# Loading four gate weights before the last blocks of a down projection, and spreading a norm's row one block later

## The chip, the cores and the metric

The kernel runs on one core of a Trainium2 chip. The metric is device time in microseconds, the median of repeated executions. Five engines work beside each other, each through its own queue in order: PE (TensorE) multiplies matrices, DVE (VectorE) and ACT (ScalarE) work on vectors, POOL (GpSimd) adds, and SP (SyncE) issues the transfers between HBM and the on-chip memory. An instruction waits until what it needs has been produced on the other engines, and everything behind it in the same queue waits with it.

## The reference, cut to what matters

One decoder layer on x of 1024 tokens by 1024 features: a gated feed-forward block, a token mixer (a short convolution and a windowed attention, each with a sigmoid gate), a second feed-forward block, and a last norm. The place of the change is the seam between the first block and the mixer:

```python
h = modulate(rms_norm(x, g_ffn1[l]), sh1, sc1)
x = x + 0.5 * gt1[:, None, :] * swiglu(h, w1_gu[l], w1_down[l])

h = modulate(rms_norm(x, g_mix[l]), sh2, sc2)
proj = h @ w_in[l]
b_g, c_g, u, q, k, v, z_conv, z_attn = jnp.split(proj, IN_OFFSETS, axis=-1)
...
merged = jax.nn.sigmoid(z_conv) * y_conv + jax.nn.sigmoid(z_attn) * y_attn
```

The norm needs the mean square over all 1024 features of a token, so it can be finished only when the last row block of x has been updated.

## The kernel before, in words

**Layout.** Features lie on the 128 partitions, tokens along the free axis. x is kept as 8 row blocks (db = 0..7) by 2 halves of 512 tokens (h = 0, 1), each a 128x512 tile. Every matrix product is done in float32 precision with three passes over split operands: each operand is cut into a rounded high part and the remainder, and `mm3` issues high by high (L138), high by low (L140) and low by high (L142). A split costs one ACT instruction for the high part (CAST, L106) and one DVE subtraction for the remainder (L107), for every 128x512 piece. Large products use a scheme of seven products in place of eight; their matmuls all stand at L195.

**Weights.** `load_w` loads a 128x1024 block into one of four raw buffers ("wr", L114) and splits it into two parts tiles, two CASTs and two L107. Parts tiles come from a pool of eight ("w"), or, where a list of tiles is handed over, from the large pool of 28 tiles ("t") that also holds the inputs of the products. A raw buffer is free for the next load when both of its halves are split.

**The seam.** After `down_seven` has done 20 of the 22 row blocks of the down projection w1_down, `down_part` does the last two for each half h: eight blocks db of six matmuls each, every one followed on DVE by `add_gated` (L569), which adds the block into x. `end1` follows each: ACT squares the block (L312 for the first, L315 for the others), POOL sums the squares (L319), and SP writes the block to HBM ("spill"). When the first half is summed, `rstd` adds over the partitions with four tiny matmuls (L328), and computes the reciprocal root on ACT and DVE (L253 to L260). `spread` turns the result into a 128x512 row with four more (L269). Both are called while PE is in the blocks of the second half: the statistic after db = 3, the row after db = 4. `mix_h` then makes the mixer's input for eight blocks: a DVE multiplication (L275), the high part and the full value on ACT (L279, L285) and the low part on DVE (L290).

**The four plain gates.** Four of the sixteen gate tiles are computed plainly, by `some_gates`: first all four on half 0 (`k` runs over the 8 input blocks; 4 x 3 matmuls for each k), then on half 1. In the first of these loops the statistic of half 1 is asked for at k = 2 and its row at k = 4, and `mix_h` for half 1 follows. Their four weight blocks are loaded by `load_w` just ahead of `some_gates` in the text. After them the first `seven_stream` begins, whose weights are split by `seven_weights` (L154 to L163 make sums of blocks, L106 and L107 split them), and which takes in blocks of the adaLN computation (L225, each on a raw buffer of its own load of "wada").

**Order.** PE's instructions are issued in the order of the text. Those of DVE, ACT, POOL and SP around the seam are ordered by a scheduler, which also hands out the buffers.

Of the kernel before, what the change touches and what calls it, by code (L numbers as in the profile page):

```python
# [35 lines left out]
def tile_macaron_layer(  # L36
# [32 lines left out]
    def nm(s):  # L69
        uid[0] += 1  # L70
        return f"{s}_{uid[0]}"
# [7 lines left out]
    def tile_t(dt=F32R, shape=(P, 2, HALF)):  # L79
        return act.tile(list(shape), dt, tag="T", name=nm("t"), bufs=28)  # L80
# [31 lines left out]
    def load_st(src):  # L112
        st = wgt.tile([P, 1024], F32, tag="wr", name=nm("wr"), bufs=4)
        nc.sync.dma_start(st[:, : src.shape[1]], src)  # L114
        return st
# [15 lines left out]
    def load_w(src, lo_engine=nc.vector, tiles=None):  # L131
        return Weights(load_st(src), src.shape[1], lo_engine, tiles)
# [132 lines left out]
    def spread(rr):  # L265

        pb = bank()
        for b in range(rr.shape[1]):
            mm(pb[:, b * P : (b + 1) * P], rr[:, b : b + 1].to_broadcast([P, P]), ident,  # L269
               start=True, stop=True)  # L270
        return pb
# [360 lines left out]
    with tc.tile_pool(name="f1", bufs=2) as tmp:  # L632
# [158 lines left out]
        def mix_h(pb, db, h):  # L791
            tt[db][h] = tile_t()
            hh2[db][h], hl2[db][h] = pair_of(tt[db][h])
            modulated(xT[db][h], pb, 1, db, hh2[db][h], hl2[db][h], xT[db][h])
            if h == 1 and db < 4:
                nc.sync.dma_start(h12[db], f32(tt[db][h]))

        wd_ = [load_w(w1d[2 * NCH, dq]) for dq in range(2)]

        def end1(h):  # L800
            def after(db):
                stats[h].add(xT[db][h])
                nc.sync.dma_start(spill[db][h], xT[db][h])
                if h == 1 and db == 3:
                    rs[0] = stats[0].rstd()
                if h == 1 and db == 4:
                    pb = spread(rs[0])
                    for d in range(KT):
                        mix_h(pb, d, 0)
            return after  # L810
# [91 lines left out]
            def c21(self, oa):  # L902
                self.done(self.i2, 0, oa, -1.0)


        plain = [(1, 0), (1, 1), (0, 0), (0, 1)]
        wg = [load_w(wz[which, db]) for which, db in plain]

        def some_gates(idx, h, between=lambda k: None):
            banks = [bank() for _ in idx]  # L910
# [514 lines left out]
```

## Time and profile before

| | before |
|---|---|
| median of 3 runs | 2264.24 us (2263.83 to 2266.13) |
| the profiled execution, whole time | 2263.03 us |
| its span in the profile | 2261.3 us |
| PE busy | 2196.2 us, 97% of the span |
| DVE busy | 1680.0 us, 74% |
| ACT busy | 1061.2 us, 47% |
| POOL busy | 382.3 us, 17% |
| the seam: last down blocks and plain gates | from 671.5 to 752.6 us of the span |

A row of a timeline gives the start and the length in microseconds, the engine, the line of the kernel, the instruction, what it writes and reads, how many were merged into the row (x3), and in brackets how long the engine had been idle before it and who ended that idle time. Matmuls overlap in the pipeline: a 128x512 matmul is shown 0.39 us long, and the next one starts 0.23 us after it. Rows of the windows view give, for a stretch of time, the busy time of each engine with its number of instructions, and behind POOL the clock that was granted to PE (1.00 is full), the share of the DMA engines and the rate.

### The profile page before, as it was taken

The page shows a single profiled execution, that of the slowest core. Times are in us where ns is not written, and L with a number is a line of the kernel's source. Part 1 is how long each engine was busy: PE and PEld are TensorE (multiplying, and loading weights), DVE is VectorE, ACT ScalarE, POOL GpSimd, SP SyncE. Part 2 cuts the span into 40 slices and gives each one's busy share as a digit, 9 for nine tenths or more (in the row PEclk, how much of TensorE's full clock was granted, in tenths as well). Part 3 has the DMA queues.
Part 4 walks back from the last instruction along what each step waited for, and adds up shares of the span by engine and source line. Part 5 has one row for each costly group of instructions (what it writes and reads, how often), then busy time and mean ns, then how long its engine had stood idle before and what let it go on. Part 6 is the DMA issues. An engine that isn't in the chain of part 4 may idle for free.

```text
span 2261.3 us, 30036 instructions
## 1 busy us (share of the span) xinstructions
PE 2196.2 (97%) x10392; PEld 1842.2 (81%) x10392; DVE 1680.0 (74%) x2978; ACT 1061.2 (47%) x2091; POOL 382.3 (17%) x429
## 2 busy tenths in 40 slices
PE   5899999999998999999999999999999999999997
PEld 4688888888886888888899998888888888888886
DVE  8897778768768877777477888555786777676876
ACT  4554444444445533433476656124554444454443
POOL 3000000004553000000344333001100000002644
PEclk9999999999999999999999999999999999999998
DMA  8264456499833534543312125444243553399932
GB/s 319 79 219 165 143 203 214 159 397 314 298 102 117 177 107 145 159 140 126 125 57 65 34 91 205 125 165 149 66 142 116 181 186 122 118 331 343 342 110 75
DMA packets 146456, 380.58 MB, mean 168 GB/s; under 512 B 20352, under 2 KB 22528, under 8 KB 146304
## 3 DMA queue, kind: packets, MB, share of 16 engines
q1 hardware_dynamic: 141696, 370.28, 46.9%
q0 software_dynamic: 4608, 8.39, 2.1%
q8 instruction: 81, 1.33, 0.2%
q14 instruction: 71, 0.58, 0.1%
HBM read 269.56 MB, written 109.05 MB: 167 GB/s over the span
## 4 chain that ended last, share of the span: by engine, by line
PE 89%; DVE 7%; issue 1%; DMA 1%; ACT 1%; POOL 1%; SPq 0%; POOLq 0%; DVEq 0%; ACTq 0%
PE ps L195 63%; PE ps L138 6%; PE ps L142 6%; PE ps L140 6%; PE ps L977 1%; PE ps L975 1%; PE ps L976 1%; DVE w L107 1%; PE ps L1031 1%; DVE t L225 1%; PE ps L1074 1%; DMA wr<-in_w2d_dram 1%; DVE t L107 1%; POOL s L319 1%; DVE x L569 1%
## 5 line engine op out<-in xcount | busy, mean ns | idle before, releaser
L195 PE MATMUL ps<-t,w 128*128 128x512 f32 x6468 | 1468.6, 389 | 4.4 <-DVE r L405 3.0
L195 PEld LDWEIGHTS ps<-t,w 128*128 128x128 f32 x6468 | 1213.6, 188 | 258.8 <-DVE r L405 4.9
L106 ACT CAST w<-wr 128x512 fp32r<-128x512 f32 (+1 forms) x412 | 250.7, 613 | 480.6 <-PE ps L195 365.1
L107 DVE TENSOR_TENSOR w<-wr,w 128x512 fp32r<-128x512 f32 (+1 forms) x396 | 299.7, 764 | 136.3 <-ACT w L106 134.9
L515 POOL TENSOR_TENSOR x<-x,g 128x512 f32<-128x512 f32 x96 | 145.6, 1531 | 1060.0 <-DMA t<-hs 940.7
L106 ACT CAST w<-ws 128x512 fp32r<-128x512 f32 x231 | 143.9, 623 | 251.4 <-PE ps L195 202.7
L140 PE MATMUL ps<-t,w 128*128 128x512 f32 (+1 forms) x528 | 205.5, 389 | 4.9 <-DVE t L290 4.9
L107 DVE TENSOR_TENSOR w<-ws,w 128x512 fp32r<-128x512 f32 x231 | 161.5, 703 | 39.1 <-ACT w L106 38.6
L138 PE MATMUL ps<-t,w 128*128 128x512 f32 (+1 forms) x400 | 156.9, 392 | 6.2 <-ACT t L279 6.2
L142 PE MATMUL ps<-t,w 128*128 128x512 f32 (+1 forms) x400 | 155.0, 388 | 2.0 <-DVE w L107 2.0
L140 PEld LDWEIGHTS ps<-t,w 128*128 128x128 f32 x528 | 100.9, 191 | 27.1 <-DVE t L290 7.6
L344 DVE TENSOR_TENSOR x<-x,x 128x512 fp32r<-128x512 f32 x161 | 102.8, 688 | 3.0 <-ACT x L343 2.8
L225 DVE CUSTOM_DVE_ANT_0 wr<-wr,crow_act,v 128x1024 f32<-128x1024 f32 x56 | 71.8, 1283 | 35.9 <-DMA wr<-in_wada_dram 35.8
L343 ACT CAST x<-x 128x512 fp32r<-128x512 f32 x161 | 88.8, 623 | 19.3 <-DVE x L431 8.0
L138 PEld LDWEIGHTS ps<-t,w 128*128 128x128 f32 x400 | 76.8, 192 | 23.2 <-ACT t L279 8.9
L319 POOL TENSOR_TENSOR s<-s,q 128x512 f32<-128x512 f32 (+1 forms) x48 | 56.8, 1186 | 201.1 <-ACT q L315 199.6
L142 PEld LDWEIGHTS ps<-t,w 128*128 128x128 f32 x400 | 76.7, 192 | 17.3 <-DVE w L107 2.4
L569 DVE SCALAR_TENSOR_TENSOR x<-ps,mods,x 128x512 f32<-128x512 f32 (+1 forms) x104 | 72.8, 707 | 22.7 <-PE ps L195 12.3
L975 PE MATMUL ps<-w,t 128*128 128x384 f32 x256 | 88.2, 345 | 1.2 <-DVE vt L1000 1.2
L107 POOL TENSOR_TENSOR w<-wr,w 128x512 fp32r<-128x512 f32 (+1 forms) x16 | 21.5, 1355 | 398.6 <-ACT w L106 398.6
L977 PE MATMUL ps<-w,t 128*128 128x384 f32 x256 | 85.7, 335 | 0.0
L976 PE MATMUL ps<-w,t 128*128 128x384 f32 x256 | 85.7, 335 | 0.0
(152 smaller groups left out, 2801.7 us busy)
## 6 DMA issues: line engine op xcount, KB each, us to landing
t<-hs SPq DMA_DIRECT2D x140, 512.0 KB, 10.1
hs<-x SPq DMA_DIRECT2D x277, 256.0 KB, 4.6
wr<-in_wada_dram SPq DMA_DIRECT2D x56, 512.0 KB, 3.8
wr<-in_w1gu_dram SPq DMA_DIRECT2D x44, 512.0 KB, 4.5
wr<-in_w2gu_dram SPq DMA_DIRECT2D x44, 512.0 KB, 3.6
wr<-in_wbcu_dram SPq DMA_DIRECT2D x24, 512.0 KB, 4.1
wr<-in_w1d_dram SPq DMA_DIRECT2D x22, 512.0 KB, 7.6
wr<-in_w2d_dram SPq DMA_DIRECT2D x22, 512.0 KB, 7.5
```

Source lines behind the costliest of these rows:

```text
L106: nc.scalar.copy(hi, src)
L107: lo_engine.tensor_tensor(lo, src, f32(hi), op=ALU.subtract)
L138: mm(o, wh, xh, start=start, stop=False)
L140: mm(o, wh, xl, start=False, stop=False)
L142: mm(o, wl, xh, start=False, stop=stop)
L195: mm(o, a, b, start=first, stop=last, skip_group_check=True)
L344: nc.vector.tensor_tensor(f32r(t), t, f32(hi), op=ALU.subtract)
L515: nc.gpsimd.tensor_tensor(dst, dst, r, op=ALU.add)
L569: nc.vector.scalar_tensor_tensor(out=dst, in0=src, scalar=gate[:, db : db + 1], in1=dst if base is None else base, op0=ALU.mult, op1=ALU.add,)
L975: mm(o[:, :384], xh, wh, start=k == 0, stop=False)
L976: mm(o[:, :384], xh, wl, start=False, stop=False)
L977: mm(o[:, :384], xl, wh, start=False, stop=k == KT - 1)
```

## The change

The list of the four plain gates and their `load_w` calls stand ahead of the definition of `end1`, so they are recorded before `down_part` runs; the last two of the four are given two tiles each of the large pool "t". And the row of half 0 is spread after block db = 5 of half 1, where it was db = 4; the statistic is still taken after db = 3.

```diff
         wd_ = [load_w(w1d[2 * NCH, dq]) for dq in range(2)]
+        plain = [(1, 0), (1, 1), (0, 0), (0, 1)]
+        wg = [load_w(wz[which, db], tiles=[tile_t(), tile_t()] if i > 1 else None)
+              for i, (which, db) in enumerate(plain)]
 
         def end1(h):
             def after(db):
...
                 if h == 1 and db == 3:
                     rs[0] = stats[0].rstd()
-                if h == 1 and db == 4:
+                if h == 1 and db == 5:
                     pb = spread(rs[0])
                     for d in range(KT):
                         mix_h(pb, d, 0)
...
-        plain = [(1, 0), (1, 1), (0, 0), (0, 1)]
-        wg = [load_w(wz[which, db]) for which, db in plain]
```

The scheduler puts the moved instructions in new places on DVE, ACT and SP; POOL keeps its order, and behind about the first two products of `seven_stream` all engines stand as before. Three places matter.

On DVE, the end of the seven products and the beginning of the last down blocks, of the changed kernel. The names that start with t_56 are the parts of the third and fourth gate weight, wr_5655 and wr_5663 their raw buffers, wr_6335 the raw buffer of the first weights of `seven_stream`; x_3953 is row block 0 of half 0:

```order
L569 SCALAR_TENSOR_TENSOR x_3957<-ps_5513,mods,x_3957 128x512
L107 TENSOR_TENSOR t_5653<-wr_5655,t_5653 128x512
L569 SCALAR_TENSOR_TENSOR x_3958<-ps_5522,mods,x_3958 128x512
L107 TENSOR_TENSOR t_5654<-wr_5655,t_5654 128x512
...
L107 TENSOR_TENSOR t_5661<-wr_5663,t_5661 128x512
L107 TENSOR_TENSOR t_5662<-wr_5663,t_5662 128x512
...
L154 TENSOR_TENSOR ws_6340<-wr_6335 128x512
L569 SCALAR_TENSOR_TENSOR x_3959<-ps_5463,ngate_3951,x_3959 128x512
...
L569 SCALAR_TENSOR_TENSOR x_3953<-ps_5670,mods,x_3953 128x512
```

Before, none of these L107 stood here (the third and fourth weight were split at the statistic of half 0 and in the middle of `mix_h`), and L154 stood behind the third L569 of the last blocks. In the built program wr_5655, wr_5663 and wr_6335 are now one and the same raw buffer, used one after the other: each load waits for the second L107 of the one before it.

On DVE, the statistic of half 0; ps_5779 and ps_5811 are its sums, x_3965 and x_3966 are blocks 4 and 5 of half 1. Before:

```order
L107 TENSOR_TENSOR w_5960<-wr_5958,w_5960 128x512
L107 TENSOR_TENSOR w_5961<-wr_5958,w_5961 128x512
L254 TENSOR_SCALAR nv_5784<-ps_5779 128x4
L255 RECIPROCAL nr_5785<-nt_5786 128x4
L569 SCALAR_TENSOR_TENSOR x_3965<-ps_5793,mods,x_3965 128x512
L256 SCALAR_TENSOR_TENSOR nt_5786<-nr_5785 128x4
L259 TENSOR_TENSOR nt_5786<-nt_5786,nv_5784 128x4
L260 SCALAR_TENSOR_TENSOR nr_5785<-nt_5786,nr_5785 128x4
```

and of the changed kernel:

```order
L107 TENSOR_TENSOR w_6337<-wr_6333,w_6337 128x512
L107 TENSOR_TENSOR w_6342<-ws_6340,w_6342 128x512
L254 TENSOR_SCALAR nv_5816<-ps_5811 128x4
L255 RECIPROCAL nr_5817<-nt_5818 128x4
L161 TENSOR_TENSOR ws_6353<-ws_6348,wr_6333 128x512
L569 SCALAR_TENSOR_TENSOR x_3965<-ps_5825,mods,x_3965 128x512
L256 SCALAR_TENSOR_TENSOR nt_5818<-nr_5817 128x4
L569 SCALAR_TENSOR_TENSOR x_3966<-ps_5837,mods,x_3966 128x512
L259 TENSOR_TENSOR nt_5818<-nt_5818,nv_5816 128x4
L260 SCALAR_TENSOR_TENSOR nr_5817<-nt_5818,nr_5817 128x4
```

Two splits still stand ahead of the statistic (now of `seven_stream`'s weights), and inside it stand two instructions more: L161, and the L569 of the block that PE does later.

On DVE, between the statistic of half 1 and its modulation, of the changed kernel; nothing stood between L260 and L275 before:

```order
L260 SCALAR_TENSOR_TENSOR nr_6008<-nt_6009,nr_6008 128x4
L225 ISA wr_6493,mods<-wr_6493,crow_act,v 128x1024
L225 ISA mods 128x1
L225 ISA wr_6496,mods<-wr_6496,crow_act,v 128x1024
L225 ISA mods 128x1
L275 SCALAR_TENSOR_TENSOR u_6046<-x_3961,amod,ps_6040 128x512
```

A third L225, on wr_6490, stands ahead of the last L290 of half 0. The raw buffers wr_6490, wr_6493 and wr_6496 are one and the same, so the loads run one after the other, each behind the L225 of the one before.

## The prediction

> **What bounds the kernel now.** I read the page first: its busy times, then the chain that ended last.
>
> ```profile
> PE 2196.2 (97%) x10392; PEld 1842.2 (81%) x10392; DVE 1680.0 (74%) x2978; ACT 1061.2 (47%) x2091; POOL 382.3 (17%) x429
> PE 89%; DVE 7%; issue 1%; DMA 1%; ACT 1%; POOL 1%; SPq 0%; POOLq 0%; DVEq 0%; ACTq 0%
> ```
>
> PE sets the time, so the change is worth only what PE loses at the seam. The windows view over the seam, and over four stretches in it, shows how much that is:
>
> ```profile
> 671.50:752.63 81.13, 73.63 (x322) 59.60 (x320) 68.19 (x105) 51.11 (x87) 20.69 (x15) 0.96 0.36 127
> 691.00:694.50 3.50, 1.18 (x9) 1.18 (x10) 2.20 (x7) 0.74 (x2) 2.88 (x3) 1.00 0.40 109
> 694.50:698.00 3.50, 3.50 (x10) 2.75 (x10) 3.40 (x6) 2.62 (x5) 0.16 (x1) 0.54 0.30 115
> 708.00:711.70 3.70, 1.22 (x10) 0.79 (x8) 3.50 (x3) 0.00 (x0) 2.87 (x2) 1.00 0.30 121
> 711.70:715.10 3.40, 3.40 (x11) 2.75 (x11) 0.74 (x5) 0.26 (x1) 0.00 (x0) 0.52 0.00 0
> ```
>
> PE is idle for 81.13 - 73.63 = 7.5 us, and twice, after a stretch in which it hardly worked, its clock is half (0.54, 0.52). The timeline of PE names the waits:
>
> ```profile
> 688.30 1.05 PE L328 MATMUL ps<-ones,s 128*128 128x1 f32 x8 [0.31 <-POOL s L319]
> 693.32 1.16 PE L269 MATMUL ps<-ident,nr 128*128 128x128 f32 x8 [2.47 <-DVE nr L260]
> 700.67 0.51 PE L140 MATMUL ps<-t,w 128*128 128x512 f32 x1 [0.23 <-DVE t L290]
> 705.23 0.50 PE L142 MATMUL ps<-t,w 128*128 128x512 f32 x1 [2.00 <-DVE w L107]
> 711.00 1.13 PE L328 MATMUL ps<-ones,s 128*128 128x1 f32 x8 [2.48 <-POOL s L319]
> 713.00 0.63 PE L142 MATMUL ps<-t,w 128*128 128x512 f32 x1
> 713.42 0.63 PE L138 MATMUL ps<-t,w 128*128 128x512 f32 x1
> 719.06 1.05 PE L269 MATMUL ps<-ident,nr 128*128 128x128 f32 x8
> 752.63 22.60 PE L195 MATMUL ps<-t,w 128*128 128x512 f32 x99
> ```
>
> The change aims at the 2.47 (the row of half 0) and the 2.00 (the split of the fourth gate weight). The wait behind them, 2.48 until 711.00, is for the statistic of half 1. Between 719.06 and 752.63 PE waits no more. So everything depends on when that second statistic can start: a wait that goes away ahead of 711.00 is only waited out there. A full-speed matmul takes 22.60/99 = 0.228 us, so a block of six is 1.37; at half clock the step is 713.42 - 713.00 = 0.42, and some eight such matmuls behind each low stretch cost 8 x 0.2 = 1.6.
>
> **The chain to the second statistic.** From the row of half 0 it runs over L275 on DVE, eight pairs on ACT, the last squares on ACT, and their sums on POOL:
>
> ```profile
> 694.60 4.70 DVE L275 SCALAR_TENSOR_TENSOR u<-x,amod,ps 128x512 f32<-128x512 f32 x7 [1.33 <-PE ps L269]
> 695.38 0.72 ACT L279 ACTIVATE t<-u,mods 128x512 fp32r<-128x512 f32 x1 [2.13 <-DVE u L275]
> 705.02 1.67 ACT L315 ACTIVATE q<-x 128x512 f32<-128x512 f32 x3
> 705.78 5.17 POOL L319 TENSOR_TENSOR s<-s,q 128x512 f32<-128x512 f32 x3 [11.12 <-ACT q L315]
> ```
>
> From 693.32 to 711.00 that is 17.68 us, and PE's own work is shorter. Three sums stand at its end, 5.17/3 = 1.72 each.
>
> **The change part by part.**
>
> *The splits in front of the last blocks.* Four L107 and four CASTs now run while the seven products end, with three more DVE instructions (L154, L158, L163). Nothing is added to the total; what counts is when L154 lets x go on.
>
> ```profile
> 655.83 0.68 DVE L107 TENSOR_TENSOR w<-wr,w 128x512 fp32r<-128x512 f32 x1
> 656.54 0.33 SPq L114 DMA_DIRECT2D wr<-in_wz_dram  x1
> DMA to landing us min/median/max: 3.4/3.6/3.8
> 661.34 1.17 DVE L107 TENSOR_TENSOR w<-wr,w 128x512 fp32r<-128x512 f32 x1
> 666.11 2.99 POOL L515 TENSOR_TENSOR x<-x,g 128x512 f32<-128x512 f32 x2 [2.45 <-DVE x L569]
> 673.14 0.75 DVE L569 SCALAR_TENSOR_TENSOR x<-ps,mods,x 128x512 f32<-128x512 f32 x1
> 676.95 0.96 DVE L154 TENSOR_TENSOR ws<-wr 128x512 f32<-128x512 f32 x1 [0.40 <-DMA wr<-in_wz_dram]
> 681.23 3.48 DVE L569 SCALAR_TENSOR_TENSOR x<-ps,mods,x 128x512 f32<-128x512 f32 x5
> 682.84 10.02 POOL L319 TENSOR_TENSOR s<-s,q 128x512 f32<-128x512 f32 x7 [2.08 <-ACT q L315]
> ```
>
> Three loads follow each other in one raw buffer. wr_5655 is issued at 656.54 as the load in its place was, and lands 3.6 later, at 660.1. Its CASTs (two, 0.6 each) and its two L107, of 1.17 each beside POOL and with an L569 between them, end at about 663.6. wr_5663 then lands at 667.3, and its splits end at about 669.7. wr_6335 is issued then and lands at 673.4. L154, L158, L163, two L569 and one L107 stand ahead of x_3953: six times 0.66 gives 677.4, against 673.14 before. POOL's last instructions for the seven products lie ahead of that. The blocks of x then go 0.66 us apart, the first square is summed from about 679.5, and seven sums of 1.33 end at 688.8. Before, four sums of 1.33 from 682.84 ended at 688.2. So the statistic starts **0.6 us later**. PE does not stall on its accumulators ahead of that: block 8 (682.4) needs the one that x_3953 frees at 678.1. Bounds: none, if the loads take 3.4; 2 us, if each of the three takes 0.4 more and the L107 beside POOL 0.3 more.
>
> *The row after db = 5.*
>
> ```profile
> 688.70 3.03 DVE L107 TENSOR_TENSOR w<-wr,w 128x512 fp32r<-128x512 f32 x2
> 691.65 0.15 DVE L254 TENSOR_SCALAR nv<-ps 128x4 f32<-128x4 f32 x1
> 693.10 0.16 DVE L260 SCALAR_TENSOR_TENSOR nr<-nt,nr 128x4 f32<-128x4 f32 x1
> ```
>
> Again two L107 hold DVE until 691.65 (at 1.5 each beside POOL), so the 0.6 us of the statistic are hidden: ACT's root would be ready at 691. Then L161 comes in (0.7 alone, 1.4 beside POOL, whose sums for half 1 still run), and L569 of block 5, which PE ends at 688.9 + 0.9 + 2 x 1.37 = 692.6. L260 ends at 694.1 to 695.0; I take 694.9, as POOL is busy. PE has then waited about 2.3 us, nearly the 2.47 of before, and L269 comes at 695.0, **1.7 us later** than 693.32, with 1.37 us more of PE's work behind it.
>
> *From the row to the second statistic.* The x of block 5 is already there, so two squares are left behind the eight pairs instead of three: 17.68 - 1.72 = 15.96, and 695.0 + 15.96 = 710.96. **The second statistic starts at 710.96 against 711.00.** With the lower end of L260 (694.1) it is 710.1; with the loads at their upper end 712.
>
> *The removed wait.* With the fourth weight split early, PE does not stop at L142. It starts k = 0 when L290 of block 0 has run: seven L275 from 696.3, one L569 and L290 give 702.3, where it was 700.67. k = 0 and 1 are 24 matmuls, 5.5 us, to 707.7. The 2.00 us are gone, and PE waits 3.2 us for the statistic instead of 2.48.
>
> *The clock.* There are now two long pauses, 698.7 to 702.3 and 707.7 to 711. If the first one halves the clock, k = 0 and 1 take 1.6 us longer, in time that is waited out anyway, the second pause is 1.6 us and may leave the clock full: 1.6 us won. If not, the second halves it as before. I count half of it, **-0.8 us**, with 0 and -1.6 as its ends. [...]
>
> *L225 ahead of the second modulation.*
>
> ```profile
> 706.36 5.13 DVE L290 SCALAR_TENSOR_TENSOR t<-u,mods,t 128x512 fp32r<-128x512 f32 x3
> L225 DVE CUSTOM_DVE_ANT_0 wr<-wr,crow_act,v 128x1024 f32<-128x1024 f32 x56 | 71.8, 1283 | 35.9 <-DMA wr<-in_wada_dram 35.8
> wr<-in_wada_dram SPq DMA_DIRECT2D x56, 512.0 KB, 3.8
> 720.15 5.36 DVE L275 SCALAR_TENSOR_TENSOR u<-x,amod,ps 128x512 f32<-128x512 f32 x8 [6.85 <-PE ps L269]
> ```
>
> The first L225 stands ahead of the last L290 of half 0, which ended at 706.36 + 5.13 = 711.5 before; I put it at 711.3 to 712.6. Then load (3.8), L225 (1.3), load, L225: 12.6 + 2 x 5.1 = 722.8, where L275 could start at 720.15. The first low part of half 1 (5.36 and 0.75 later) is there at 728.9; PE reaches half 1 at 719.9 + 48 x 0.228 = 730.8. So 2.7 us late are hidden under 4.6; without that cover they would cost one for one. Behind it DVE has as much left as before, and `seven_stream`'s first weights are split already.
>
> **Sum.** -0.04 for the second statistic and -0.8 for the clock: **-0.8 us**. The profiled execution (2263.03, span 2261.3) becomes 2262.2. It is 1.2 below the median of the runs, 2264.24, so the median becomes **2263.4**. Its own range: -0.9 - 1.6 at the best, +1 with late loads and +1.6 for a second slow stretch, rounded to 2261 to 2267.
>
> **Rivals.** One: *the removed waits are a gain as they stand*, 2.47 + 2.00 + 2.48 and one slow stretch of 1.6, 8.5 us: 2255.7. For it speaks that all of them are on the chain of PE; against it, that the second statistic starts from the row of half 0, and that two instructions now stand inside that row's computation. Chance 0.05. Two: *serial loads hold DVE*. Three loads in one raw buffer stand ahead of the first statistic, two ahead of the second modulation. It decides from the point where the first three are over 1 us late in sum (the cover that L254 gives), or the two over 1.9. With the 7.6 us that the page gives for a load beside heavy traffic,
>
> ```profile
> wr<-in_w1d_dram SPq DMA_DIRECT2D x22, 512.0 KB, 7.6
> ```
>
> it is 3 x 4.0 - 1 = 11 us: 2275. Against it: the loads of in_wz here took 3.8 at most, and the DMA share of the whole seam is 0.36. Chance 0.06. Three: *the change does not do what it says*: the row moves by a block of PE's work, 1.37 us, two splits still stand ahead of the statistic, and the wait at L142 is only moved; the chain then ends 1.4 later: 2265.6. Chance 0.12. The forecast keeps 0.77.
>
> **How the numbers follow.** A measurement of this kernel tells 0.2%, 4.5 us, from no change. The forecast and rival three lie within it. Faster takes rival one and 0.01 of the rest, 0.06; slower is 0.05, most of rival two; the same, 0.89. Eight in ten lie from 2260.5 to 2267.0: the forecast's own range with half a microsecond for the runs below it, and rival three inside.
>
> **What would show it.** L142's wait for L107 at the gates is gone. The two CAST and L107 pairs of the third and fourth weight lie ahead of 671.5. L154 waits for its load until about 673.4, and x_3953 follows at 677. L269 of half 0 starts at 694 to 695.5, with a wait of 1.5 to 2.4 us. PE then waits about 3.5 us for L290, and once more for POOL at L328, which starts at 710 to 712. The second L275 starts at 722 to 723.5, and PE does not wait for it. Wrong would be: L328 ahead of 708, or PE idle after 719, or a load of the seam over 4.5 us.

## The result and the profile after

The changed kernel takes **2268.81 us** (median of 22 runs, 2266.30 to 2274.26) against 2264.60 us of the kernel before, in as many runs beside it. The ratio is 1.0020, with a 95% interval of 1.0014 to 1.0027: the change costs 3 to 6 us. The prediction was 2263.4 us and no difference that can be told. The profiled execution has a span of 2267.2 us, 5.9 us more than before.

By the page of the changed kernel PE is busy for 2196.8 us, as before (2196.2). Its share of the chain that ended last falls from 89% to 87%, DMA goes from 1% to 2% and DVE from 7% to 8%:

```profile
PE 87%; DVE 8%; DMA 2%; issue 1%; ACT 1%; POOL 1%; SPq 0%; POOLq 0%; DVEq 0%; ACTq 0%
```

The timeline of PE at the seam, changed kernel: its four waits of over 0.3 us, the tiny matmuls of the statistics (L328) and rows (L269), and the first product of `seven_stream` behind the seam:

```profile
671.13 3.04 PE L195 MATMUL ps<-t,w 128*128 128x512 f32 x12 [3.00 <-DVE x L569]
690.33 0.95 PE L328 MATMUL ps<-ones,s 128*128 128x1 f32 x8
697.38 2.08 PE L269 MATMUL ps<-ident,nr 128*128 128x128 f32 x8 [3.22 <-DVE nr L260]
705.64 0.50 PE L140 MATMUL ps<-t,w 128*128 128x512 f32 x1 [2.57 <-DVE t L290]
714.88 1.87 PE L328 MATMUL ps<-ones,s 128*128 128x1 f32 x8 [3.72 <-POOL s L319]
724.28 1.05 PE L269 MATMUL ps<-ident,nr 128*128 128x128 f32 x8
757.84 22.38 PE L195 MATMUL ps<-t,w 128*128 128x512 f32 x98
```

The first row is new: 3.00 us in which PE, ahead of the last twelve matmuls of the seven products, waits for DVE to add a block into x. The 2.00 us at L142 are gone, as the change meant, but the waits for the row and for the second statistic have grown from 2.47 to 3.22 and from 2.48 to 3.72.

To compare executions, times are taken from one event ahead of the seam, an addition of DVE in the seven products, some 60 us earlier. Before and after:

```profile
612.91 1.40 DVE L569 SCALAR_TENSOR_TENSOR x<-ps,ngate,x 128x512 f32<-128x512 f32 x2
```
```profile
612.32 1.40 DVE L569 SCALAR_TENSOR_TENSOR x<-ps,ngate,x 128x512 f32<-128x512 f32 x2
```

From there to the first product of `seven_stream` it was 752.63 - 612.91 = 139.72 us, and is 757.84 - 612.32 = 145.52: **5.8 us more, nearly the whole of the 5.9 that the span gained**. (These are two single executions; the medians lie 4.2 us apart.) Cut at the starts of L328 and L269, the parts were 75.39 to the first statistic, 5.02 to its row, 17.68 to the second statistic, 8.06 to its row, and 33.57 to the end. The change moved them by +2.62, +2.03, -0.18, +1.34 and -0.01.

**The first loss.** The chain of waits of the changed kernel shows what stands behind the 3.00 us (start, length, and the engine or transfer that the chain runs through):

```profile
663.21 3.51 DMA wr<-in_wz_dram
666.79 0.63 ACT t L106
667.45 1.07 DVE t L107 x2
668.73 1.01 issue
669.74 0.68 DVE w L107
670.42 0.67 DVE x L569
671.13 3.04 PE ps L195 x12
```

The load of the fourth weight, the second of the three that share one raw buffer, lands at 666.7. Its splits hold DVE until 669.7, a split of the first weight stands behind them, and only then comes L569, which reads a sum out of an accumulator bank. The last twelve matmuls (q4) add onto this bank and its neighbour, so they must not start before the sum has been read; this is what is meant below where an instruction empties or frees a bank. Before, it ran at 667.87 and ended at 668.61, and PE did not stop:

```profile
667.87 0.74 DVE L569 SCALAR_TENSOR_TENSOR x<-ps,ngate,x 128x512 f32<-128x512 f32 x1
```

**The second loss.** DVE in the computation of the row of half 0, changed kernel:

```profile
691.20 1.79 DVE L107 TENSOR_TENSOR w<-wr,w 128x512 fp32r<-128x512 f32 x1
692.91 0.68 DVE L107 TENSOR_TENSOR w<-ws,w 128x512 fp32r<-128x512 f32 x1
693.51 0.15 DVE L254 TENSOR_SCALAR nv<-ps 128x4 f32<-128x4 f32 x1
693.67 0.65 DVE L161 TENSOR_TENSOR ws<-ws,wr 128x512 f32<-128x512 f32 x1
694.25 0.73 DVE L569 SCALAR_TENSOR_TENSOR x<-ps,mods,x 128x512 f32<-128x512 f32 x1
694.91 0.56 DVE L256 SCALAR_TENSOR_TENSOR nt<-nr 128x4 f32<-128x4 f32 x1
695.39 0.74 DVE L569 SCALAR_TENSOR_TENSOR x<-ps,mods,x 128x512 f32<-128x512 f32 x1
696.05 1.08 DVE L259 TENSOR_TENSOR nt<-nt,nv 128x4 f32<-128x4 f32 x1
```

The chain from L254 to L260 took 693.10 - 691.65 = 1.45 us before, with one L569 in it; with L161 and a second L569 it is 3.7 us (693.51 to 697.17). PE pauses longer, and L269 then runs at half clock: 2.08 us in place of 1.16. The windows view (clock: the third number from the end) shows the window behind the new 3.00 us first, then L269 and the stretch behind the second statistic, whose half clock lasts until 721:

```profile
671.10:674.50 3.40, 3.37 (x15) 2.77 (x16) 3.07 (x3) 0.29 (x1) 2.99 (x2) 1.00 0.79 304
697.40:700.00 2.60, 2.60 (x10) 2.50 (x11) 0.43 (x1) 0.00 (x0) 1.06 (x1) 0.50 0.11 40
716.00:720.00 4.00, 4.00 (x12) 3.32 (x13) 2.38 (x8) 0.26 (x1) 0.00 (x0) 0.50 0.38 131
```

### The profile page after: what moved, and what is told of

It reads as the page before. It is cut to its first block, busy times and chain, and to the rows that moved or that the text cites. A ratio compares the mean times of both kernels' runs of the same rounds, so it can differ in the third digit from the quotient of the medians.

```text
span 2267.2 us, 30032 instructions
## 1 busy us (share of the span) xinstructions
PE 2196.8 (97%) x10392; PEld 1843.3 (81%) x10392; DVE 1679.3 (74%) x2978; ACT 1062.2 (47%) x2091; POOL 381.8 (17%) x429
## 4 chain that ended last, share of the span: by engine, by line
PE 87%; DVE 8%; DMA 2%; issue 1%; ACT 1%; POOL 1%; SPq 0%; POOLq 0%; DVEq 0%; ACTq 0%
PE ps L195 61%; PE ps L138 6%; PE ps L140 6%; PE ps L142 6%; PE ps L977 2%; PE ps L976 2%; PE ps L975 2%; DVE w L107 1%; PE ps L1031 1%; PE ps L1074 1%; DVE t L225 1%; DMA wr<-in_w2d_dram 1%; DVE x L569 1%; POOL s L319 1%; DVE u L275 1%
## 5 line engine op out<-in xcount | busy, mean ns | idle before, releaser
L195 PE MATMUL ps<-t,w 128*128 128x512 f32 x6468 | 1469.0, 389 | 7.7 <-DVE x L569 4.5
L195 PEld LDWEIGHTS ps<-t,w 128*128 128x128 f32 x6468 | 1213.5, 188 | 262.7 <-DVE x L569 5.4
L107 DVE TENSOR_TENSOR w<-wr,w 128x512 fp32r<-128x512 f32 (+1 forms) x392 | 295.4, 760 | 138.7 <-ACT w L106 137.2
L140 PE MATMUL ps<-t,w 128*128 128x512 f32 (+1 forms) x496 | 192.5, 388 | 7.2 <-DVE t L290 7.2
L107 DVE TENSOR_TENSOR w<-ws,w 128x512 fp32r<-128x512 f32 x231 | 160.5, 699 | 42.0 <-ACT w L106 41.5
L138 PE MATMUL ps<-t,w 128*128 128x512 f32 (+1 forms) x368 | 143.8, 391 | 6.3 <-ACT t L279 6.2
L142 PE MATMUL ps<-t,w 128*128 128x512 f32 (+1 forms) x368 | 141.8, 385 | 0.0
L140 PEld LDWEIGHTS ps<-t,w 128*128 128x128 f32 x496 | 94.5, 191 | 27.9 <-DVE t L290 9.9
L225 DVE CUSTOM_DVE_ANT_0 wr<-wr,crow_act,v 128x1024 f32<-128x1024 f32 x56 | 72.8, 1301 | 41.6 <-DMA wr<-in_wada_dram 41.6
L569 DVE SCALAR_TENSOR_TENSOR x<-ps,mods,x 128x512 f32<-128x512 f32 (+1 forms) x104 | 72.8, 707 | 25.0 <-PE ps L195 13.1
L107 POOL TENSOR_TENSOR w<-wr,w 128x512 fp32r<-128x512 f32 (+1 forms) x16 | 21.5, 1355 | 400.1 <-ACT w L106 400.1
L138 PEld LDWEIGHTS ps<-t,w 128*128 128x128 f32 x368 | 70.5, 192 | 22.1 <-ACT t L279 9.0
L142 PEld LDWEIGHTS ps<-t,w 128*128 128x128 f32 x368 | 70.4, 191 | 13.3
```

Of the source, the lines that this page charges most:

```text
L107: lo_engine.tensor_tensor(lo, src, f32(hi), op=ALU.subtract)
L138: mm(o, wh, xh, start=start, stop=False)
L140: mm(o, wh, xl, start=False, stop=False)
L142: mm(o, wl, xh, start=False, stop=stop)
L195: mm(o, a, b, start=first, stop=last, skip_group_check=True)
L225: nc.vector.tensor_tensor_reduce(out=st, in0=st, in1=crow_act, scale=1.0, scalar=v[:, C_BADA + i : C_BADA + i + 1], op0=ALU.mult, op1=ALU. ...
```

## The experiments

Three theories stood at first. **A**: the loads that follow each other in one raw buffer hold DVE in front of the L569 that frees PE's bank. **B**: the later row is the loss in itself. **C**: the early loads cost by their traffic, wherever they stand. All runs were cut into the same five parts; the table gives their differences from before, in us, from one profiled execution each, and the ratio of the median times to the kernel before, each measured beside it.

| run | to 1st L328 | to L269 | to 2nd L328 | to L269 | to the end | sum | ratio (95% interval) |
|---|---|---|---|---|---|---|---|
| the change | +2.62 | +2.03 | -0.18 | +1.34 | -0.01 | +5.80 | 1.0020 (1.0014 to 1.0027) |
| loads alone | +2.63 | +0.57 | -0.04 | +2.02 | +0.01 | +5.19 | 1.0023 (1.0010 to 1.0036) |
| row alone | 0.00 | +0.01 | -0.72 | +0.03 | 0.00 | -0.68 | 0.9993 (0.9985 to 1.0002) |
| own raw tiles | +5.36 | +2.04 | -1.04 | +0.03 | -0.01 | +6.38 | 1.0029 (1.0020 to 1.0038) |
| own raw tiles, row after db = 4 | +3.30 | +0.57 | -0.04 | +1.99 | 0.00 | +5.82 | 1.0029 (1.0020 to 1.0038) |
| no third and fourth weight | +3.08 | +0.57 | +0.10 | +1.64 | -0.01 | +5.38 | 1.0023 (1.0013 to 1.0034) |
| low parts on POOL | +0.98 | +1.81 | -0.20 | +1.03 | -0.01 | +3.61 | 1.0009 (1.0000 to 1.0018) |
| bank emptied by ACT | +1.48 | +1.96 | -1.09 | +0.02 | -0.01 | +2.36 | 1.0010 (1.0001 to 1.0019) |
| row alone, ask later | +0.01 | +0.01 | -0.69 | +0.04 | -2.72 | -3.35 | 0.9989 (0.9980 to 0.9998) |
| the same, last square on PE | 0.00 | +0.01 | -1.29 | -0.78 | -2.72 | -4.78 | 0.9978 (0.9969 to 0.9987) |

### One: each half of the change alone

The loads alone (the change with the row moved back):

```diff
-                if h == 1 and db == 5:
+                if h == 1 and db == 4:
                     pb = spread(rs[0])
```

> The four weights early, the row of half 0 after db = 4 as before. Theory A (the serial loads in one raw buffer hold DVE in front of the accumulators that PE needs): PE's wait of 3.0 us at L195, put down to DVE x L569, stays, and the first statistic (L328) is 2.6 us later than before. Its other half, theory B (the later row costs 2.0 us between L328 and L269, and the longer pause 1.3 us of clock), falls away: 2264.6 + 2.6 = about 2267. If B is the whole loss, it comes out at 2264.6; if A is, at 2268.8.

Measured: 2268.66 us. PE in this run:

```profile
671.62 3.02 PE L195 MATMUL ps<-t,w 128*128 128x512 f32 x12 [3.02 <-DVE x L569]
696.39 1.16 PE L269 MATMUL ps<-ident,nr 128*128 128x128 f32 x8 [3.13 <-DVE nr L260]
714.03 1.87 PE L328 MATMUL ps<-ones,s 128*128 128x1 f32 x8 [4.79 <-POOL s L319]
```

The loads alone make nearly the whole loss; the time did not fall to 2267. They keep the wait at L195, and also the wait for the row, since one more instruction of `seven_stream`'s weights (L161) stands inside its computation. The wait for the second statistic is 4.79 us: the sum of the 2.48 and 2.00 of before and 0.3. So the time that PE no longer loses at L142 is waited out for POOL.

The row alone (the kernel before with the row after db = 5):

```diff
-                if h == 1 and db == 4:
+                if h == 1 and db == 5:
                     pb = spread(rs[0])
```

> The loads as before, the row of half 0 after db = 5. Theory A: no wait at L195. On DVE nothing has come in ahead of L260, so L269 stays at 693.3 and waits 2.47 - 1.37 = 1.1 us; two squares are left behind the pairs in place of three, one L569 stands ahead of L275: the second statistic comes 1.0 us earlier, the wait at L142 stays. 2263 to 2264. Theory B (the later row by itself is the loss): 2.0 + 1.3 us slower, 2267.9.

Measured: 2262.28 us beside 2263.37; the interval of the ratio runs from 0.9985 to 1.0002, so the loss that B had forecast is ruled out, and a gain isn't shown.

PE in this run, and POOL's last sums:

```profile
693.46 1.16 PE L269 MATMUL ps<-ident,nr 128*128 128x128 f32 x8 [1.12 <-DVE nr L260]
710.42 1.05 PE L328 MATMUL ps<-ones,s 128*128 128x1 f32 x8 [3.11 <-POOL s L319]
```
```profile
705.91 4.46 POOL L319 TENSOR_TENSOR s<-s,q 128x512 f32<-128x512 f32 x2 [9.67 <-ACT q L315]
```

Theory B falls as it stood. The wait of 1.12 and the unmoved L269 came as expected, the second statistic 0.7 us earlier in place of 1.0: two sums stand behind the pairs in place of three, but take 2.23 us each (4.46 against 5.17 for three). One thing was expected wrong: the wait at L142 is gone without the early loads, because the scheduler now puts the split of the fourth weight two L290 earlier. The 2.03 us that the row's computation costs in the change are an interaction: L161 stands in front of L259 only with the loads moved (+0.57 in the loads alone), and the second L569 only with both moved; with the row alone it stands behind L260.

### Two: raw tiles of their own

```diff
+        def load_own(src):
+            st = tile_c(F32)
+            nc.sync.dma_start(st, src)
+            return st
-        wg = [load_w(wz[which, db], tiles=[tile_t(), tile_t()] if i > 1 else None)
-              for i, (which, db) in enumerate(plain)]
+        wg = [Weights(load_own(wz[which, db]), tiles=[tile_t(), tile_t()]) if i > 1
+              else load_w(wz[which, db]) for i, (which, db) in enumerate(plain)]
```

> The change, but the raw data of the third and fourth weight stand in tiles of their own, so that no two of the loads share a buffer there. Theory A: no wait at L195, all behind it 2.6 to 3.0 us earlier: 2265.8 to 2266.2; the waits at L269 and L328 stay as in the change (3.2 and 3.7 us). Theory C (the early loads and splits cost by their traffic and their place on DVE, not by the shared buffer): the wait at L195 stays, 2268.8.

> As the run with raw tiles of its own, and the row after db = 4 as before. A and B add up: 2268.8 - 2.8 - 3.3 = 2262.7, no wait at L195 and none at L142; PE waits for the row as before (2.5) and for the second statistic. If only A is right: 2266. If the later row was a gain in itself: later than the run with raw tiles of its own.

Measured: 2269.62 us and 2270.21 us, where A had 2266 and 2263. Without the chain of loads PE still stops, and in a second place too. PE with the row after db = 5, and the same place with the row after db = 4:

```profile
634.33 35.66 PE L195 MATMUL ps<-t,w 128*128 128x512 f32 x156 [1.19 <-DVE x L569]
672.64 4.24 PE L195 MATMUL ps<-t,w 128*128 128x512 f32 x12 [2.65 <-DVE x L569]
```
```profile
672.50 3.01 PE L195 MATMUL ps<-t,w 128*128 128x512 f32 x12 [2.65 <-DVE x L569]
```

Both runs were expected several us faster than they are. Theory A in its narrow form falls: the shared buffer isn't needed for the stall. Free raw tiles let the third and fourth weight be split earlier still, ahead of another L569 at 634; and since the four raw buffers are free sooner, `seven_stream`'s first weight is loaded sooner too, and the scheduler puts its sums (L154, L158, L163) in front of the L569 that before ran ahead of them. This led to theory **D**: work on DVE ahead of the L569 that empties a bank stops PE as soon as it holds that L569 beyond the time at which PE needs the bank, be it a split that waits for a load or a sum that only takes its time.

### Three: without the third and fourth weight

The four splits and two loads are left out; the third and fourth gate are computed with the first and second weight again.

```diff
-        wg = [load_w(wz[which, db], tiles=[tile_t(), tile_t()] if i > 1 else None)
-              for i, (which, db) in enumerate(plain)]
+        wg = [load_w(wz[which, db]) for which, db in plain[:2]]
+        wg += wg
```

(and the row after db = 4.)

> As the run with raw tiles of its own and the row after db = 4, but the third and fourth weight are neither loaded nor split: their products take the first and second weight again, so the output is another one. Theory D: what holds x L569 behind the seven products is seven_stream's first weight, whose sums (L154, L158, L163) come ahead of it as soon as the two raw buffers are free: PE's wait of 2.65 us at L195 near 672.5 stays although four splits are gone, and only the 0.75 us near 634 goes away; 0.7 us below the run with them, 2269. Theory A: the four splits themselves are the cause; no wait at L195, 2266.

Measured: 2268.71 us. PE's row, and DVE ahead of it:

```profile
671.34 3.02 PE L195 MATMUL ps<-t,w 128*128 128x512 f32 x12 [3.48 <-DVE x L569]
```
```profile
665.36 1.73 DVE L154 TENSOR_TENSOR ws<-wr 128x512 f32<-128x512 f32 x1 [0.25 <-DMA wr<-in_wz_dram]
667.02 0.74 DVE L569 SCALAR_TENSOR_TENSOR x<-ps,mods,x 128x512 f32<-128x512 f32 x1
667.68 0.68 DVE L107 TENSOR_TENSOR w<-wr,w 128x512 fp32r<-128x512 f32 x1
668.28 1.75 DVE L158 TENSOR_TENSOR ws<-ws,wr 128x512 f32<-128x512 f32 x1
669.95 0.68 DVE L163 TENSOR_TENSOR wr<-wr,wr 128x512 f32<-128x512 f32 x1
670.55 1.40 DVE L569 SCALAR_TENSOR_TENSOR x<-ps,ngate,x 128x512 f32<-128x512 f32 x2
```

With no third and fourth weight at all PE waits as long (3.48 where 2.65 was expected). Three sums have come in ahead of the L569: 1.73 + 1.75 + 0.68 = 4.2 us of DVE, more than the wait. The wait at 634 is gone with the splits, as expected. The splits of the moved weights are thus not the only cause, freed buffers do it too: a raw buffer that is free sooner lets the next load in line, and the work on it, come sooner.

### Four: take the work, or the bank, off DVE

The change with the low parts of the third and fourth weight on POOL:

```diff
-        wg = [load_w(wz[which, db], tiles=[tile_t(), tile_t()] if i > 1 else None)
+        wg = [load_w(wz[which, db], nc.gpsimd if i > 1 else nc.vector,
+                     tiles=[tile_t(), tile_t()] if i > 1 else None)
```

> The change, with the low parts of the third and fourth weight on POOL in place of DVE. Neither L107 nor L154 then stands ahead of the L569 that frees the bank. Theory D and A alike: no wait at L195, L328 of half 0 at 688 to 689, L269 7.05 later as in the change: 2268.8 - 2.7 = 2266. If POOL's use beside DVE is what makes the seam slow, the wait stays or moves to another L569, and it is 2268 or more.

The change with the two banks emptied by ACT, everything else where it was:

```diff
             for s in range(2):
                 product(oa[s], w["q7"], t["q7"], cols[s], False, True)
                 m2 = base + 2 + s
+                if n == len(steps) - 1:
+                    g = scaled_copy(oa[s], ngate, m2)
+                    nc.vector.tensor_tensor(xs[m2][1], xs[m2][1], g, op=ALU.add)
+                    nc.gpsimd.tensor_tensor(xs[m2][1], xs[m2][1], r[5, s], op=ALU.add)
+                    continue
                 gather(xs[m2][1], oa[s], r[5, s], ngate, m2, c == 0)
```

> The change, and in the last step of the seven products the two banks that PE's last twelve matmuls need are emptied by ACT (a scaled copy into scratch) in place of DVE's L569; DVE adds the copy instead, in the same place of its queue. Loads, splits and orders stay. Theory D (PE waits because the instruction that empties the bank stands behind other work in DVE's queue): ACT has the copy behind the two CASTs of the fourth weight, which end near 668.1, so the bank is free near 669.5 and PE's wait falls from 3.0 to about 1.3 us, put down to ACT: 2267. If something else holds PE there (traffic, the weight load, PE's own queue), it stays at 3.0.

Measured: 2266.43 us and 2266.59 us, both about 0.1% over before. PE with the low parts on POOL, then PE and ACT with the bank emptied by ACT:

```profile
670.14 3.01 PE L195 MATMUL ps<-t,w 128*128 128x512 f32 x12 [0.95 <-DVE x L569]
```
```profile
669.68 3.01 PE L195 MATMUL ps<-t,w 128*128 128x512 f32 x12 [0.86 <-ACT g L570]
```
```profile
667.38 1.14 ACT L106 CAST t<-wr 128x512 fp32r<-128x512 f32 x2 [2.71 <-DMA wr<-in_wz_dram]
668.43 0.61 ACT L106 CAST w<-wr 128x512 fp32r<-128x512 f32 x1
668.95 1.26 ACT L570 ACTIVATE g<-ps,ngate 128x512 f32<-128x512 f32 x2
```

The second of these is the decisive run for D. Loads and splits are those of the change, DVE's queue has the same order up to that place (behind it L154 and two splits stand a little otherwise), and another engine empties the bank; the wait falls from 3.00 to 0.86 us and is now put down to ACT, where the copy stands behind the casts of the same load. That shows it: PE waits for a bank, and the bank waits in a queue. It also ends theory C for this wait, as the loads are the same.

With the low parts on POOL the time is near the 2266 that was expected, but 0.95 us of the wait are left where none was. The trace shows what holds the bank there:

```profile
666.89 1.14 ACT L106 CAST t<-wr 128x512 fp32r<-128x512 f32 x2 [1.84 <-DMA wr<-in_wz_dram]
```
```profile
668.58 0.85 DVE L107 TENSOR_TENSOR w<-wr,w 128x512 fp32r<-128x512 f32 x1 [1.17 <-ACT w L106]
```

The L569 stands on DVE behind the split of the first weight, and the cast for that split stands on ACT (at 667.93) behind the two casts of the fourth weight, which wait for their load. It is the same mechanism, one engine further on.

With either cure the first statistic is still 1.0 to 1.5 us late and the row's computation still costs 1.8 to 2.0 us. In both runs L328 waits for POOL's sums again, 0.28 and 0.86 us: behind PE's stall lies the later start of the sums, which comes from x_3953 being late.

### Five: fill the wait

The longest wait of PE in the kernel with the row alone is the 3.11 us for the second statistic. So it is asked for later:

```diff
-            if k == 2:
+            if k == 3:
                 rs[1] = stats[1].rstd()
-            if k == 4:
+            if k == 5:
                 pb = spread(rs[1])
```

> The row alone after db = 5, the loads as before the change, and in the gates of half 0 the second statistic is asked for at k = 3 and its row at k = 5 (2 and 4). The 12 matmuls of k = 2, 2.74 us, fill the wait of 3.11 us for POOL, so 0.4 is left, and with no long pause the clock stays full, 1.5 us: 2.7 + 1.5 = 4.2 us below the run with the row alone, 2258 to 2259. If the second modulation becomes the bound, PE waits at the first matmuls of half 1 and the gain is under 2 us.

Measured: 2261.52 us, 0.02 to 0.2% under before. The seam is 2.7 us shorter than with the row alone, of the 4.2 expected:

```profile
709.89 1.05 PE L328 MATMUL ps<-ones,s 128*128 128x1 f32 x8 [1.76 <-POOL s L319]
```

The second row comes at the same distance behind it (717.99), but only three blocks k of twelve matmuls follow it now, where there were four. A wait of 1.76 was left where 0.4 was expected, as the clock had stayed full in k = 0 and 1 (1.00 from 699.6 to 703.2 and from 704 to 708; 0.70 from 700 to 704 and 0.83 from 704 to 707 with the row alone) and PE came there sooner; behind it the clock was halved (0.51 from 711.6 to 715.0), once in this seam, where it is halved twice with the row alone (0.73 from 710 to 714 the second time). The second modulation did not become the bound.

Then POOL's last sum is taken out of the chain: PE adds the last square by itself.

```diff
-            stats[h] = Stats()
+            stats[h] = Stats(fold=h == 0)
```

> The row alone after db = 5 with the second statistic asked for at k = 3 and its row at k = 5, and for half 1 the last square is not summed by POOL but by PE with four more small matmuls. POOL's last sum, 1.7 to 2.0 us, falls out of the chain to the second statistic: PE's wait of 1.76 us for POOL falls under 0.3 us, and without that pause the clock stays full behind it (1.5 us): 3 us below the run with the later statistic alone, 2258.5. If the halved clock hangs on the first pause instead, only the 1.7 us: 2260.

Measured: **2259.70 us, ratio 0.9978 (0.9969 to 0.9987)**: faster than both kernels, by 3 to 7 us against the one before.

```profile
700.75:704.16 3.41, 3.41 (x10) 2.64 (x9) 3.41 (x6) 3.41 (x7) 0.00 (x0) 0.50 0.23 82
708.00:716.00 8.00, 8.00 (x45) 6.89 (x44) 0.73 (x5) 0.26 (x1) 0.32 (x1) 1.00 0.00 0
```

PE no longer waits at L328 (709.10), and is busy at full clock (1.00) for the 8 us around it. But a halved stretch has not been saved, it has moved: it now lies behind the first pause, from 700.75 (0.50). So this run took the second of the two ways that were expected (2260): by the table the seam is 1.4 us shorter than in the run before it, not 3. PE's waits left in this seam are 0.30, 1.14 and 2.55 us, for the first statistic, its row and the first L290.

## Why the prediction was wrong

**The step that failed** is a sentence under the splits in front of the last blocks: "PE does not stall on its accumulators ahead of that". The working had set out the times of the chain of loads, and they were close. With the 0.59 us added by which this execution ran ahead, the fourth weight's load was put at 667.3 and landed at 667.3, L154 was put at 673.4 and came at 673.9, x_3953 at 677.4 and came at 678.3. But the working looked only at the banks of the last down blocks. The L569 of x_3967 (block 6 of half 1), which stands behind those very L107 and which the working does not name, empties the bank that the last twelve matmuls need first. Its end near 671 followed from the same times, and was never held against PE, which had done the matmuls ahead at 668.1 (671.13 less the 3.00 of the wait). The statistic of half 0 thus came 2.62 us later, not 0.6: PE's own work was late, and L328 no longer waited for POOL at all.

The 0.6 was too small for the chain through POOL as well:

```profile
679.95 10.79 POOL L319 TENSOR_TENSOR s<-s,q 128x512 f32<-128x512 f32 x8 [5.80 <-ACT q L315]
```

The first sum was put at 679.5 and came at 680.5 with the 0.59 added; seven of these eight sums, at 1.35 each, end at 690.0, where 688.8 was forecast. By that estimate the statistic would have been 1.7 us late without PE's stall; with the bank emptied by ACT it was 1.48 late. So the stall and the late sums overlap, and curing the stall alone wins about 1.1 of the 2.62.

**The row after db = 5** was put 1.7 us later, of which 0.6 for the statistic was hidden; L269 came 2.62 + 2.03 = 4.65 us later. The two instructions inside the computation had been read from the order, and the price of each was about right (0.65 and 0.74). What was oversized is the cover: the chain behind L254 starts from a PE that is 2.6 us late, so nothing was hidden. And L259, 0.16 us before (at 692.91, with POOL's sum ended at 692.85), took 1.08 at 696.05 while POOL added beside it (from 695.85 to 698.46).

**From the row to the second statistic** the prediction took off a whole sum of 1.72 us. It was -0.18, so the second statistic came 4.47 us later, not 0.04 sooner. One sum did go, but L269 itself took 0.9 us more on the halved clock (2.08 in place of 1.16), and the two sums left took 4.05 us, 2.0 each. In the run with the row alone, where L269 ran at full clock (1.16 us; 1.00 from 690 to 698), the gain was 0.72, as the two sums took 2.23 each.

**The clock** was counted at -0.8 with ends at 0 and -1.6. In this execution it was a loss: the pause of 2.57 us at L140, which was to take the halved clock, left it full (1.00 from 705.6 to 709.5); at the row and the second statistic it was halved as before (0.50 from 697.4 to 700 and from 716 to 720; 0.54 and 0.52 before), and the second stretch was 6.8 us long, from 714.3 to 721.1, where it was 3.4, from 711.8 to 715.2 (the part behind the second statistic grew by 1.34). That a shorter second pause, of 1.6 us, would leave the clock full was an estimate; in the run that asks later 1.76 us were followed by half clock (0.51). With the 4.47 this makes the 5.8 us.

**Right were** the removed wait at L142, which was only waited out (3.72 us for POOL, 4.79 with the loads alone), and the two L225 ahead of the second modulation. They end as L275 starts, at 725.57, 1.3 us behind the row, and PE does not wait: the last part of the seam, 33.56 us, is as before (L275 started 1.1 us behind the row then):

```profile
724.36 1.28 DVE L225 CUSTOM_DVE_ANT_0 wr<-wr,crow_act,v 128x1024 f32<-128x1024 f32 x1 [3.63 <-DMA wr<-in_wada_dram]
```

**The rivals.** The second, serial loads that hold DVE, had the right place and was given 0.06, as its point of decision was set at loads over 1 us late. No load was late; it was enough that they came on time, one after the other, in front of the wrong instruction. The first rival fell. The third was right in one part: the wait was moved.

## What to carry to other kernels

An instruction that is put ahead of another in an in-order queue must be weighed against whoever waits for what stands behind it. For an engine that also empties accumulators that is the matmul engine, and the time to compare with is when it next needs that bank, not when the block itself is needed. A load or split moved earlier also frees its buffer earlier, and a scheduler may then pull unrelated work forward: read the order where nothing was edited. A wait for a late value can be filled by asking for it one block of independent matmuls later: here two changed numbers took 2.7 us off the seam.

## What was not expected of the hardware

**The length of a pause did not settle whether the clock was halved.** In the changed kernel PE stood still for 3.00 us ahead of 671.13 and for 2.57 us ahead of 705.64, and the clock was full behind both (granted clock 1.00 from 671.1 to 674.5 and from 705.6 to 709.5). The two runs with raw tiles of their own stop for the same 2.65 us at the same place; the twelve matmuls behind it took 4.24 us in one (granted clock 0.68 from 672.6 to 676.9) and 3.01 in the other. In the run that asks later, a pause of 1.76 us at 709.89 was enough (0.51 from 711.6 to 715.0). What else decides is not shown: no run moved a pause on purpose and left the rest as it was. So a term for the clock can't be sized from the pause alone, and the +1.34 above belongs to one execution.

**DVE beside POOL.** In the traces of the two kernels, from 600 to 760 us of the span, additions and subtractions of 128x512 on DVE (TENSOR_TENSOR) took 0.68 to 0.70 us where no addition of POOL overlapped them, and 0.65 to 1.80 where one did: in the changed kernel the L107 at 692.91 took 0.68 without POOL, the one at 691.20 took 1.79 beside POOL's sum from 691.14 to 692.44, and L161 at 693.67 only 0.65, though POOL's next sum began at 693.75. So an overlap alone did not make each of them slow. L259, on 128x4 elements, took 1.08 at 696.05 beside POOL's sums, and 0.16 in the same kernel at 717.57, where POOL was idle; in the loads alone, at 695.97, it took 0.16. That POOL makes the difference is read from which rows overlap; no run took POOL's work away to show it.
